# Block sums of the second layer's FFN weights: formed one layer earlier and kept in DRAM

## The chip, the cores and the metric

One core of a Trainium2 chip. The time of a run is in microseconds (us) of device time. TensorE (PE) multiplies; its weight loads stand as PEld. VectorE (DVE) and GpSimd (POOL) do elementwise work, ScalarE (ACT) copies, converts and evaluates functions, and SyncE (SP) issues all transfers of this kernel, in the order of its queue.

## The reference, cut to what matters

Two layers over 512 latent tokens and 256 context tokens of width 1024, all in float32. A layer is token mixing (four groups of heads) and a SwiGLU FFN of hidden width 2816; the context stream runs only in the first layer's FFN. The change is about the FFN of the second layer, for the latent tokens:

```
def swiglu(h, w_in_, w_out_):
    gate, up = jnp.split(h @ w_in_, 2, axis=-1)
    return (jax.nn.silu(gate) * up) @ w_out_
...
x = x + g_f * rms_norm(swiglu(modulate(rms_norm(x, norm_g[2]), sh_f, sc_f), w_ffn_in, w_ffn_out), norm_g[3])
```

`w_ffn_in` is 1024 x 5632 per layer, `w_ffn_out` 2816 x 1024. The vectors `sh_f`, `sc_f` and their like come from six products of the conditioning with `w_mod` (the modulation).

## The kernel before, in words

Features lie on the 128 partitions and tokens on the free axis. Every weight tile is split into a rounded part `wh` (ACT, line 408) and its remainder `wl` (POOL or DVE, line 409), activations likewise, and one block product is three matmuls (`mac3`, lines 470 to 472: wh with high, wh with low, wl with high). A weight unit is 128 x 1024 numbers (512 KB): `weights` (line 414) calls `tick`, takes a raw tile from the ring `wr` (5 buffers), issues its load on SP (line 425) and splits it in two halves into the rings `wh` and `wl` (5 buffers each). The 2816 hidden columns are 22 blocks j of 128, each with a gate tile (u = 0) and an up tile (u = 1) in `wfi`.

First layer, latent tokens (`ffn`): chunks of 8, 7 and 7 blocks; per block two units, then 8 units of `w_ffn_out` (wfo) per chunk, the last 6 of the last chunk in halves of the tokens. Beside it run background tasks: `mix` (line 1907) fills the queue `bg` with 32 tasks of `mods_sums` (the second layer's modulation, line 659: a 512 KB load at line 667 and two DVE operations at line 675 or 677 each) and sets `bg_rate` to `rate2`; each `tick` adds the rate and runs a task whenever a whole one has come together. What is left is flushed when the layer's last normalisation begins.

Second layer, latent tokens (`ffn_seven`): blocks 0 to 3 go as above; the other 18 are made by `strassen_pair` (line 1541). It takes the gate and up columns of a block as the two rows, and the two halves of the 1024 inputs as the two columns, of a 2 x 2 block matrix A = (a11 a12; a21 a22) of 128 x 512 each, and the two halves of the tokens and inputs as the other matrix. In place of eight block products it makes seven, with the sums of A formed on the spot from the two raw tiles (line 1553, helper `tt`): s1 = a21 + a22 and a21 = a11 - a21 on POOL, s2 = s1 - a11 and a12 = a12 - s2 on DVE (`sad` is 'PPVV'). Products 0, 2, 4 and 6 add into one PSUM tile, Z; between them Z is read, by ACT after product 0 (line 1579) and 2 (line 1583) and by DVE after product 4 (line 1587, tile `fd`). The sums of the other matrix are made once, in `strassen_rhs` (lines 1513 to 1539). Each product's block is split into wh and wl as it comes.

The chunks of blocks in the second layer are (0, 4), (4, 7), (7, 11), (11, 16) and (16, 22). While a chunk's products run, the 8 output tiles of the chunk before (`ffn_tiles`, wfo units from the ring `wq` of 2) are put between them; before, they are spread evenly: after each product, as many are made as keep step.

The order in which each engine's instructions run is set when the kernel is built, by a planner that goes by program order as priority and by its own estimates of durations; the engines then keep that order and wait on semaphores. Tiles of the arena (`main.get`) are 67 slots that are handed on in the order in which they are freed.

Of the kernel before, what the change touches and what calls it, by code (L numbers as in the profile page):

```python
# [11 lines left out]
F32 = mybir.dt.float32  # L12
# [5 lines left out]
ALU = mybir.AluOpType  # L18
# [3 lines left out]
P = 128  # L22
D = 1024
KT = D // P
# [3 lines left out]
HID = 22  # L28
# [9 lines left out]
 'netmp': 3,  # L38
 'nmain': 36,
 'nctx': 26,  # L40
 'wr': 5,
 'wh': 5,
 'wl': 5,
 'fcx': ((0, 8), (8, 15), (15, 22)),
# [19 lines left out]
 'latei': 2,  # L64
 'rate0': 0.8,
 'rate1': 0.2,
 'rate2': 0.5,
 'lo': ('4', '4', '6', '3', '2', '4', '5', '3', '4'),
 'sqk': 'VPVPVPVP',
 'sqe': 'AAAAAAAA',  # L70
# [38 lines left out]
 'strassen': (1,),  # L109
 'fcs': ((0, 4), (4, 7), (7, 11), (11, 16), (16, 22)),  # L110
 'fco': 4,
 'wq': 2,
 'sad': 'PPVV',
 'slo': 'PVVPPVP',
# [1 line left out]
 'srt': 'VPVP',  # L116
 'srl': 'VPVP',
 'sup': 'V',
 'sgl': 'V',
 'ws': 4}  # L120
UNIT = 1024
HALF = 544
NEG = -1e30
# [139 lines left out]
class Build:  # L263
    def __init__(self, tc, es, I, out, dbg=None):
        self.tc, self.nc, self.I, self.out, self.dbg = tc, tc.nc, I, out, dbg
        pool = lambda name, **k: es.enter_context(tc.tile_pool(name=name, **k))
        self.cp = pool("const", bufs=1)
        self.pp = pool("param", bufs=1)
        self.sp = pool("small", bufs=1)
        self.wr = pool("wr", bufs=T["wr"])  # L270
        self.wh = pool("wh", bufs=T["wh"])
        self.wl = pool("wl", bufs=T["wl"])
        self.ws = pool("ws", bufs=T["ws"])
# [12 lines left out]
        self.modrow = Arena(self.sp, "modrow", 1)  # L286
        self.bg = deque()
        self.pre = deque()
# [1224 lines left out]
    def strassen_rhs(self, h):  # L1513
# [24 lines left out]
        h.blocks = [[b11], [b21, b22]]  # L1538
        return out, [b11, b21, out[1], out[0], out[2], b22, out[3]]

    def strassen_pair(self, l, j, h, rhs, g, jj):

        nc = self.nc
        n = h.half
        raw = []
        for u in range(2):
            self.tick()
            r = self.wr.tile([P, UNIT], F32, tag="wr", name=self.name("wr"))
            nc.sync.dma_start(out=r.rearrange("p (a b) -> p a b", a=KT), in_=self.I["wfi"][l, j, u])
            raw.append(r)  # L1550
        a11, a12, a21, a22 = raw[0][:, 0:512], raw[0][:, 512:1024], raw[1][:, 0:512], raw[1][:, 512:1024]
        s1, s2 = (self.ws.tile([P, 512], F32, tag="ws", name=self.name("ws")) for _ in range(2))
        tt = lambda c, o, a, b, op: self.e(c).tensor_tensor(out=o, in0=a, in1=b, op=op)  # L1553
        ad = T["sad"]
        tt(ad[0], s1, a21, a22, ALU.add)
        tt(ad[1], a21, a11, a21, ALU.subtract)
        tt(ad[2], s2, s1, a11, ALU.subtract)
        lhs = [a11, a12, s2, s1, a21, a12, a22]
        z, w, y = self.mm(), None, None
        c1 = self.ar.temp("fc", 2 * n)  # L1560
        c2 = self.ar.temp("fd", n)
        e = self.ar.temp("fe", 2 * n)
        p5 = self.ar.temp("ff", n)
        c1t, c2t, p1, q, p5t = c1.t[:, 0:2 * n], c2.t[:, 0:n], e.t[:, 0:n], e.t[:, n:2 * n], p5.t[:, 0:n]
        for i in range(7):
# [2 lines left out]
            self.split(hi, lo, lhs[i], eng=self.e(T["slo"][i]))  # L1568
            if i == 1:
                y = self.mm()  # L1570
                tt(ad[3], a12, a12, s2, ALU.subtract)
# [26 lines left out]
        tt(T["sup"], a[:, n:2 * n], a[:, n:2 * n], c2t, ALU.mult)  # L1598
# [18 lines left out]
    def ffn_seven(self, l, st, h, G, chunks, first, hold, last, hold2, then, between, after):  # L1617
# [3 lines left out]
        n = st.n  # L1621
# [27 lines left out]
        for ci, (k0, k1) in enumerate(rest):  # L1649
            outs = self.ffn_tiles(l, y, g, j0, j1, KT, n, sq, ci == 0, False, self.mx)  # L1650
            ahead = 0 if ci else T["fco"]
            for _ in range(ahead):
                next(outs)
            gn = HL(self.ar, "g", k1 - k0, n)
            total, done = 7 * (k1 - k0), 0
            for i, _ in enumerate(self.strassen_tiles(l, k0, k1, h, rhs, gn)):
                while done * total < (i + 1) * (KT - ahead):
                    next(outs)
                    done += 1
            self.all(outs)  # L1660
            g.free()
            g, j0, j1 = gn, k0, k1
# [162 lines left out]
    def run(self):  # L1825
# [81 lines left out]
        def mix():  # L1907
            self.ar = side
            self.ctx_states(C, pn)
            main.absorb(side)  # L1910
            main.other, self.tmp.lends = self.tmp, True
            self.ar = main
            self.mods_sums(1, (2, 4, 3, 5), pn, 1)
            self.bg_rate = T["rate2"]

        self.layer_end(0, X, p, pn, norm, proj, mix)
# [162 lines left out]
```

## Time and profile before

| what | value |
|---|---|
| median of 3 runs | 1700.4 us (1699.37 to 1701.58) |
| the profiled execution | 1700.72 us |
| its span, first to last instruction | 1698.9 us |
| PE, DVE, ACT, POOL busy | 95%, 65%, 46%, 44% of the span |
| moved by DMA | 219.41 MB, mean 129 GB/s |
| chain that ended last | PE 13%, DVE 3%, issue 2%, POOL 2%, ACT 1% |

The profile is one execution. Busy time is the union of an engine's instructions; matmuls are pipelined and overlap in it. A wait is idle time of an engine ahead of an instruction, put down to what released it. The name left of an arrow is the tile that is written, right of it what is read; L is the line in the kernel. The first layer's FFN for the latent tokens runs from some 645 to 1046 us, the second layer's from 1311 us to the end, its seven products from some 1371 to 1657 us.

### The profile page before, as it was taken

What the parts mean: (1) busy time and instruction counts of PE and PEld (TensorE: products, weight loads), DVE (VectorE), ACT (ScalarE), POOL (GpSimd) and SP (SyncE); (2) the same over time, 40 slices, a digit from 0 to 9 for tenths busy, and PEclk for the clock granted to TensorE, in tenths of its full rate; (3) what the DMA queues carried; (4) which work ended last, traced back from release to release, by engine and by line L of the source; (5) the groups of instructions that cost most, each with busy time, mean ns of one, the idle gap of its engine ahead of it and who ended that gap; (6) DMA issues with size and microseconds to landing.
All of it is one profiled execution on the core that took longest, in us unless ns stands there. A gap on an engine that the chain in (4) does not pass through costs nothing. (4 is left out here: it accounts for less than half of the span.)

```text
span 1698.9 us, 28931 instructions
## 1 busy us (share of the span) xinstructions
PE 1605.5 (95%) x10616; PEld 1402.3 (83%) x10616; DVE 1095.9 (65%) x2330; ACT 787.5 (46%) x1782; POOL 748.9 (44%) x779
## 2 busy tenths in 40 slices
PE   6999998999999998999999997999698999999997
PEld 2976777887899998888888887999478988889886
DVE  4876675758785668643443556758756857677874
ACT  3655356554345545333322333464465344444451
POOL 2431334554466555322222224332425766676663
PEclk9999999899999999999999998999799999999998
DMA  9654553354475323344434453121032123333242
GB/s 312 228 174 160 202 192 118 109 174 153 124 246 180 122 87 102 125 148 137 140 122 147 148 188 97 54 75 63 1 125 88 63 80 97 105 106 106 77 124 69
DMA packets 85663, 219.41 MB, mean 129 GB/s; under 512 B 11025, under 2 KB 20113, under 8 KB 85521
## 3 DMA queue, kind: packets, MB, share of 16 engines
q1 hardware_dynamic: 85520, 217.57, 39.6%
q8 instruction: 83, 1.36, 0.3%
q14 instruction: 60, 0.48, 0.1%
HBM read 211.24 MB, written 6.29 MB: 128 GB/s over the span
## 5 line engine op out<-in xcount | busy, mean ns | idle before, releaser
L409 POOL TENSOR_TENSOR wl<-wr,wh 128x512 fp32r<-128x512 f32 (+2 forms) x250 | 335.9, 1349 | 505.6 <-ACT wh L408 487.3
L408 ACT ACTIVATE wh<-wr 128x512 fp32r<-128x512 f32 (+3 forms) x512 | 310.4, 617 | 452.6 <-PE mm L471 320.5
L409 DVE TENSOR_TENSOR wl<-wr,wh 128x512 fp32r<-128x512 f32 (+3 forms) x262 | 218.7, 838 | 127.5 <-ACT wh L408 125.5
L470 PE MATMUL mm<-hfh_m,wh 128*128 128x512 f32 (+1 forms) x320 | 125.0, 391 | 0.0
L472 PE MATMUL mm<-hfh_m,wl 128*128 128x512 f32 (+1 forms) x320 | 124.8, 390 | 0.0
L471 PE MATMUL mm<-hfl_m,wh 128*128 128x512 f32 (+1 forms) x320 | 124.5, 389 | 0.0
L471 PE MATMUL mm<-hfl_c,wh 128*128 128x256 f32 x352 | 100.8, 287 | 0.6 <-POOL hfl_c L582 0.6
L472 PE MATMUL mm<-hfh_c,wl 128*128 128x256 f32 x352 | 100.6, 286 | 0.0
L470 PE MATMUL mm<-hfh_c,wh 128*128 128x256 f32 x352 | 100.1, 285 | 0.0
L472 PEld LDWEIGHTS mm<-hfh_m,wl 128*128 128x128 f32 x320 | 60.5, 189 | 13.5
L471 PEld LDWEIGHTS mm<-hfl_m,wh 128*128 128x128 f32 x320 | 60.4, 189 | 13.0
L470 PEld LDWEIGHTS mm<-hfh_c,wh 128*128 128x128 f32 x352 | 66.7, 190 | 5.3 <-issue 2.3
L470 PEld LDWEIGHTS mm<-hfh_m,wh 128*128 128x128 f32 x320 | 60.4, 189 | 12.9
L471 PEld LDWEIGHTS mm<-hfl_c,wh 128*128 128x128 f32 x352 | 66.8, 190 | 2.0 <-POOL hfl_c L582 0.8
L472 PEld LDWEIGHTS mm<-hfh_c,wl 128*128 128x128 f32 x352 | 67.0, 190 | 1.6 <-issue 0.6
L677 DVE SCALAR_TENSOR_TENSOR macc_m<-wr,cs,macc_m 128x512 f32<-128x512 f32 x56 | 43.0, 767 | 29.6 <-DMA wr<-in_wmod_dram 28.6
L471 PE MATMUL mm<-gl_m,wh 128*128 128x512 f32 x152 | 59.8, 394 | 0.0
L472 PE MATMUL mm<-gh_m,wl 128*128 128x512 f32 x152 | 59.7, 394 | 0.0
L470 PE MATMUL mm<-gh_m,wh 128*128 128x512 f32 x152 | 59.6, 396 | 0.0
L470 PE MATMUL mx<-gh_m,wh 128*128 128x512 f32 x128 | 50.7, 399 | 3.3 <-ACT wh L408 2.2
L472 PE MATMUL mx<-gh_m,wl 128*128 128x512 f32 x128 | 50.9, 398 | 1.6 <-POOL wl L409 1.2
L471 PE MATMUL mx<-gl_m,wh 128*128 128x512 f32 x128 | 50.5, 394 | 0.0
(725 smaller groups left out, 5420.9 us busy)
## 6 DMA issues: line engine op xcount, KB each, us to landing
wr<-in_wfi_dram SPq DMA_DIRECT2D x132, 512.0 KB, 3.8
wr<-in_wmod_dram SPq DMA_DIRECT2D x80, 512.0 KB, 4.1
wr<-in_wT_dram SPq DMA_DIRECT2D x42, 512.0 KB, 3.9
wr<-in_wo_dram SPq DMA_DIRECT2D x24, 512.0 KB, 3.9
wr<-in_wfo_dram SPq DMA_DIRECT2D x24, 512.0 KB, 4.0
wm_m<-in_wmod_dram SPq DMA_DIRECT2D x32, 256.0 KB, 5.2
wr<-in_wfo_dram SPq DMA_DIRECT2D x16, 448.0 KB, 3.8
wr<-in_wfo_dram SPq DMA_DIRECT2D x16, 384.0 KB, 3.4
```

The costliest lines, as they stand in the source:

```text
L408: nc.scalar.activation(hi, src, AF.Copy)
L409: (eng or nc.vector).tensor_tensor(out=lo, in0=src, in1=hi.bitcast(F32), op=ALU.subtract)
L470: nc.tensor.matmul(out, lh, rh, start=first, stop=False, skip_group_check=more)
L471: nc.tensor.matmul(out, lh, rl, start=False, stop=False, skip_group_check=more)
L472: nc.tensor.matmul(out, ll, rh, start=False, stop=last, skip_group_check=more)
L677: nc.vector.scalar_tensor_tensor(out=t, in0=w, scalar=self.cs[:, k, s:s + 1], in1=t, op0=ALU.mult, op1=ALU.add)
```

## The change

The first layer's FFN gets 36 more background tasks (`weight_sums`), put evenly among the 32 of the modulation, and `rate2` is 1.4 in place of 0.5. A task loads the four 128 x 512 blocks of a hidden block j (four transfers of 256 KB into arena slots), or forms the four sums (as before two on POOL and two on DVE) and stores them to a DRAM tile (four transfers of 256 KB); the load of j + 1 stands ahead of the forming of j. In the second layer a pair loads four tiles: a11 and a12 (512 KB), s2 and s1, a21 and a12 from DRAM (512 KB each) and a22 (256 KB), in the order in which the products use them, and forms nothing. The ring `wr` has 7 buffers in place of 5; the ring `ws` of the sums (4 buffers of half the size) goes. The output tiles between the products stand at fixed places: a pair that is due one has it behind product 5, a second one behind product 1, a third behind product 3.

```
--- before.py
+++ after.py
@@ -38,7 +38,7 @@
  'netmp': 3,
  'nmain': 36,
  'nctx': 26,
- 'wr': 5,
+ 'wr': 7,
  'wh': 5,
  'wl': 5,
  'fcx': ((0, 8), (8, 15), (15, 22)),
@@ -64,7 +64,7 @@
  'latei': 2,
  'rate0': 0.8,
  'rate1': 0.2,
- 'rate2': 0.5,
+ 'rate2': 1.4,
  'lo': ('4', '4', '6', '3', '2', '4', '5', '3', '4'),
  'sqk': 'VPVPVPVP',
  'sqe': 'AAAAAAAA',
@@ -109,6 +109,7 @@
  'strassen': (1,),
  'fcs': ((0, 4), (4, 7), (7, 11), (11, 16), (16, 22)),
  'fco': 4,
+ 'fcp': (5, 1, 3),
  'wq': 2,
  'sad': 'PPVV',
  'slo': 'PVVPPVP',
@@ -116,8 +117,7 @@
  'srt': 'VPVP',
  'srl': 'VPVP',
  'sup': 'V',
- 'sgl': 'V',
- 'ws': 4}
+ 'sgl': 'V'}
 UNIT = 1024
 HALF = 544
 NEG = -1e30
@@ -270,7 +270,6 @@
         self.wr = pool("wr", bufs=T["wr"])
         self.wh = pool("wh", bufs=T["wh"])
         self.wl = pool("wl", bufs=T["wl"])
-        self.ws = pool("ws", bufs=T["ws"])
         self.wq = pool("wq", bufs=T["wq"])
         self.ap = pool("arena", bufs=1)
         self.dr = pool("dram", bufs=1, space=bass.MemoryType.DRAM)
@@ -285,6 +284,7 @@
         self.ar = self.main
         self.modrow = Arena(self.sp, "modrow", 1)
         self.bg = deque()
+        self.sums = {}
         self.pre = deque()
         self.bg_rate = self.bg_acc = 0.0
         self.uid = 0
@@ -1538,24 +1538,54 @@
         h.blocks = [[b11], [b21, b22]]
         return out, [b11, b21, out[1], out[0], out[2], b22, out[3]]
 
+    def weight_sums(self, l, j0, j1):
+
+        nc = self.nc
+
+        def load(j, box):
+            for u in range(2):
+                for v in range(2):
+                    s = self.main.get("sa")
+                    nc.sync.dma_start(out=s.t[:, 0:512].rearrange("p (a b) -> p a b", b=P), in_=self.I["wfi"][l, j, u][:, v * 4:v * 4 + 4])
+                    box.append(s)
+
+        def form(j, box):
+            a11, a12, a21, a22 = (s.t[:, 0:512] for s in box)
+            box += [self.main.get("sb") for _ in range(2)]
+            s1, s2 = (s.t[:, 0:512] for s in box[4:])
+            tt = lambda c, o, a, b, op=ALU.subtract: self.e(c).tensor_tensor(out=o, in0=a, in1=b, op=op)
+            e = T["sad"]
+            tt(e[0], s1, a21, a22, ALU.add)
+            tt(e[1], a21, a11, a21)
+            tt(e[2], s2, s1, a11)
+            tt(e[3], a12, a12, s2)
+            d = self.dr.tile([P, 2, KT, P], F32, tag=f"ws{l}{j}", name=f"ws{l}{j}")
+            self.sums[l, j] = d
+            for i, x in enumerate((s2, s1, a21, a12)):
+                nc.sync.dma_start(out=d[:, i // 2, i % 2 * 4:i % 2 * 4 + 4], in_=x.rearrange("p (a b) -> p a b", b=P))
+            for s in box:
+                s.free()
+
+        boxes = {j: [] for j in range(j0, j1)}
+        tasks = [lambda: load(j0, boxes[j0])]
+        for j in range(j0, j1):
+            if j + 1 < j1:
+                tasks.append(lambda j=j: load(j + 1, boxes[j + 1]))
+            tasks.append(lambda j=j: form(j, boxes[j]))
+        return tasks
+
     def strassen_pair(self, l, j, h, rhs, g, jj):
 
         nc = self.nc
         n = h.half
         raw = []
-        for u in range(2):
+        for src in (self.I["wfi"][l, j, 0], self.sums[l, j][:, 0], self.sums[l, j][:, 1], self.I["wfi"][l, j, 1][:, KT // 2:KT]):
             self.tick()
             r = self.wr.tile([P, UNIT], F32, tag="wr", name=self.name("wr"))
-            nc.sync.dma_start(out=r.rearrange("p (a b) -> p a b", a=KT), in_=self.I["wfi"][l, j, u])
+            k = src.shape[1]
+            nc.sync.dma_start(out=r[:, 0:k * P].rearrange("p (a b) -> p a b", a=k), in_=src)
             raw.append(r)
-        a11, a12, a21, a22 = raw[0][:, 0:512], raw[0][:, 512:1024], raw[1][:, 0:512], raw[1][:, 512:1024]
-        s1, s2 = (self.ws.tile([P, 512], F32, tag="ws", name=self.name("ws")) for _ in range(2))
-        tt = lambda c, o, a, b, op: self.e(c).tensor_tensor(out=o, in0=a, in1=b, op=op)
-        ad = T["sad"]
-        tt(ad[0], s1, a21, a22, ALU.add)
-        tt(ad[1], a21, a11, a21, ALU.subtract)
-        tt(ad[2], s2, s1, a11, ALU.subtract)
-        lhs = [a11, a12, s2, s1, a21, a12, a22]
+        lhs = [r[:, i * 512:i * 512 + 512] for r in raw for i in range(2)][0:7]
         z, w, y = self.mm(), None, None
         c1 = self.ar.temp("fc", 2 * n)
         c2 = self.ar.temp("fd", n)
@@ -1568,7 +1598,6 @@
             self.split(hi, lo, lhs[i], eng=self.e(T["slo"][i]))
             if i == 1:
                 y = self.mm()
-                tt(ad[3], a12, a12, s2, ALU.subtract)
             if i == 3:
                 w = self.mm()
             ps, first = [(z, True), (y, True), (z, False), (w, True), (z, False), (w, False), (z, False)][i]
@@ -1595,7 +1624,7 @@
         nc.scalar.activation(a, c1t, AF.Tanh)
         nc.vector.scalar_tensor_tensor(out=a, in0=a, scalar=1.0, in1=c1t, op0=ALU.add, op1=ALU.mult)
         nc.vector.tensor_tensor(out=a[:, 0:n], in0=z[:, 0:n], in1=a[:, 0:n], op=ALU.mult)
-        tt(T["sup"], a[:, n:2 * n], a[:, n:2 * n], c2t, ALU.mult)
+        self.e(T["sup"]).tensor_tensor(out=a[:, n:2 * n], in0=a[:, n:2 * n], in1=c2t, op=ALU.mult)
         self.split(g.h[jj], g.l[jj], a, eng=self.e(T["sgl"]))
         for x in (c1, c2, e):
             x.free()
@@ -1652,11 +1681,11 @@
             for _ in range(ahead):
                 next(outs)
             gn = HL(self.ar, "g", k1 - k0, n)
-            total, done = 7 * (k1 - k0), 0
+            nj, left = k1 - k0, KT - ahead
             for i, _ in enumerate(self.strassen_tiles(l, k0, k1, h, rhs, gn)):
-                while done * total < (i + 1) * (KT - ahead):
+                q = (i // 7 + 1) * left // nj - i // 7 * left // nj
+                if i % 7 in T["fcp"][0:q]:
                     next(outs)
-                    done += 1
             self.all(outs)
             g.free()
             g, j0, j1 = gn, k0, k1
@@ -1911,6 +1940,10 @@
             main.other, self.tmp.lends = self.tmp, True
             self.ar = main
             self.mods_sums(1, (2, 4, 3, 5), pn, 1)
+            a, b = list(self.bg), self.weight_sums(1, T["fcs"][0][1], HID)
+            self.bg.clear()
+            for i, f in enumerate(b):
+                self.bg += a[i * len(a) // len(b):(i + 1) * len(a) // len(b)] + [f]
             self.bg_rate = T["rate2"]
 
         self.layer_end(0, X, p, pn, norm, proj, mix)
```

## Rows read from the trace of the kernel before

**Rows 1.** Page: busy time with share and count; GB/s in forty slices.

```profile
PE 1605.5 (95%) x10616; PEld 1402.3 (83%) x10616; DVE 1095.9 (65%) x2330; ACT 787.5 (46%) x1782; POOL 748.9 (44%) x779
...
GB/s 312 228 174 160 202 192 118 109 174 153 124 246 180 122 87 102 125 148 137 140 122 147 148 188 97 54 75 63 1 125 88 63 80 97 105 106 106 77 124 69
```

**Rows 2.** Stages: us; PE, PEld, DVE, ACT, POOL busy (x); PEclk, DMA share, GB/s.

```profile
20.00:30.00 10.00, 8.94 (x47) 3.51 (x45) 5.99 (x19) 1.18 (x4) 2.64 (x7) 1.00 1.05 403
800.00:900.00 100.00, 100.00 (x442) 81.42 (x441) 42.79 (x62) 30.67 (x52) 23.71 (x18) 1.00 0.42 137
900.00:1000.00 100.00, 100.00 (x441) 81.45 (x441) 48.44 (x71) 32.85 (x58) 25.13 (x19) 1.00 0.47 152
1360.00:1376.00 16.00, 13.03 (x70) 10.01 (x69) 10.06 (x10) 6.32 (x12) 11.89 (x9) 1.00 0.32 99
1376.00:1460.00 84.00, 81.79 (x578) 75.91 (x577) 56.37 (x75) 42.87 (x86) 51.07 (x38) 1.00 0.29 89
1460.00:1560.00 100.00, 96.38 (x680) 89.42 (x679) 71.89 (x97) 46.59 (x91) 68.85 (x47) 1.00 0.34 105
1560.00:1660.00 100.00, 96.71 (x654) 88.04 (x653) 75.28 (x96) 48.25 (x98) 62.61 (x44) 1.00 0.35 103
```

**Rows 3.** Waits of PE, 1360 to 1660 us: total us, times, longest.

```profile
PE mm L470 <- DVE fd_m L1587: 4.2, 5, 1.2
PE mx L470 <- ACT wh L408: 2.2, 2, 1.6
```

**Rows 4.** Waits of PE, 690 to 1010 us: the only one.

```profile
PE mx L1329 <- POOL kw_c L304: 0.2, 1, 0.2
```

**Rows 5.** Timeline, 1478 to 1483 us: start, us, operation, [idle before <- its releaser].

```profile
1478.76 1.30 POOL L1553 TENSOR_TENSOR ws<-wr 128x512 f32<-128x512 f32 x1 [1.15 <-DMA wr<-in_wfi_dram]
...
1480.09 1.76 DVE L1553 TENSOR_TENSOR ws<-ws,wr 128x512 f32<-128x512 f32 x1 [3.23 <-POOL ws L1553]
...
1481.77 0.41 DVE L1587 TENSOR_TENSOR fd_m<-mm,fd_m 128x256 f32<-128x256 f32 x1
...
1482.23 0.19 PEld L470 LDWEIGHTS mm<-st3h_m,wh 128*128 128x128 f32 x1 [1.38 <-DVE fd_m L1587]
```

**Rows 6.** Line 1553, the sums: ns min/median/max; then what they waited for (us, times).

```profile
L1553 POOL TENSOR_TENSOR ws<-wr x18: 1282/1292/1746, 1312.5 to 1616.5; 128x512 f32<-128x512 f32 x18
...
L1553 DVE TENSOR_TENSOR ws<-ws,wr x18: 676/1752/1784, 1314.0 to 1617.8; 128x512 f32<-128x512 f32 x18
...
L1553 POOL TENSOR_TENSOR wr<-wr,wr x18: 1342/1738/1803, 1315.2 to 1619.0; 128x512 f32<-128x512 f32 x18
...
L1553 DVE TENSOR_TENSOR wr<-wr,ws x18: 674/1038/1780, 1377.3 to 1634.0; 128x512 f32<-128x512 f32 x18
...
  POOL ws L1553: 33.4, 13
...
  DMA wr<-in_wfi_dram: 17.3, 13
```

**Rows 7.** Timeline of PE around 1408 us.

```profile
1407.61 0.28 PE L471 MATMUL mm<-hf10l_m,wh 128*128 128x256 f32 x1
1407.73 0.28 PE L472 MATMUL mm<-hf10h_m,wl 128*128 128x256 f32 x1
1408.59 0.38 PE L470 MATMUL mm<-st3h_m,wh 128*128 128x256 f32 x1 [0.59 <-DVE fd_m L1587]
```

**Rows 8.** DMA issues by line: count, KB each, median us to landing.

```profile
wr<-in_wfi_dram SPq DMA_DIRECT2D x132, 512.0 KB, 3.8
...
xs<-x_m SPq DMA_DIRECT2D x8, 256.0 KB, 2.1
```

**Rows 9.** SP queue: modulation loads of line 667 (first and last start); sixteen issues.

```profile
L667 SPq DMA_DIRECT2D wr<-in_wmod_dram x32: 378/378/379, 655.7 to 1000.8; - x32
...
2.57 10.38 SPq L627 DMA_DIRECT2D wm_m<-in_wmod_dram  x16
```

**Rows 10.** Waits of PE, 1010 to 1320 us: the second in size.

```profile
PE mx L1431 <- DVE ht_m L800: 7.8, 3, 3.4
```

More of the change, by code (lines that the diff above doesn't have):

```diff
@@ L40 @@
  'nctx': 26,
- 'wr': 5,
+ 'wr': 7,
  'wh': 5,
@@ L111 @@
  'fco': 4,
+ 'fcp': (5, 1, 3),
  'wq': 2,
@@ L118 @@
  'sup': 'V',
- 'sgl': 'V',
- 'ws': 4}
+ 'sgl': 'V'}
 UNIT = 1024
@@ L287, in __init__ @@
         self.bg = deque()
+        self.sums = {}
         self.pre = deque()
@@ L1539, in strassen_rhs, with weight_sums, load, form @@
         return out, [b11, b21, out[1], out[0], out[2], b22, out[3]]
+    def weight_sums(self, l, j0, j1):
+        nc = self.nc
+        def load(j, box):
+            for u in range(2):
+                for v in range(2):
+                    s = self.main.get("sa")
+                    nc.sync.dma_start(out=s.t[:, 0:512].rearrange("p (a b) -> p a b", b=P), in_=self.I["wfi"][l, j, u][:, v * 4:v * 4 + 4])
+                    box.append(s)
+        def form(j, box):
+            a11, a12, a21, a22 = (s.t[:, 0:512] for s in box)
+            box += [self.main.get("sb") for _ in range(2)]
+            s1, s2 = (s.t[:, 0:512] for s in box[4:])
+            tt = lambda c, o, a, b, op=ALU.subtract: self.e(c).tensor_tensor(out=o, in0=a, in1=b, op=op)
+            e = T["sad"]
+            tt(e[0], s1, a21, a22, ALU.add)
+            tt(e[1], a21, a11, a21)
+            tt(e[2], s2, s1, a11)
+            tt(e[3], a12, a12, s2)
+            d = self.dr.tile([P, 2, KT, P], F32, tag=f"ws{l}{j}", name=f"ws{l}{j}")
+            self.sums[l, j] = d
+            for i, x in enumerate((s2, s1, a21, a12)):
+                nc.sync.dma_start(out=d[:, i // 2, i % 2 * 4:i % 2 * 4 + 4], in_=x.rearrange("p (a b) -> p a b", b=P))
+            for s in box:
+                s.free()
+        boxes = {j: [] for j in range(j0, j1)}
+        tasks = [lambda: load(j0, boxes[j0])]
+        for j in range(j0, j1):
+            if j + 1 < j1:
+                tasks.append(lambda j=j: load(j + 1, boxes[j + 1]))
+            tasks.append(lambda j=j: form(j, boxes[j]))
+        return tasks
     def strassen_pair(self, l, j, h, rhs, g, jj):
@@ L1545, in strassen_pair @@
         raw = []
-        for u in range(2):
+        for src in (self.I["wfi"][l, j, 0], self.sums[l, j][:, 0], self.sums[l, j][:, 1], self.I["wfi"][l, j, 1][:, KT // 2:KT]):
             self.tick()
             r = self.wr.tile([P, UNIT], F32, tag="wr", name=self.name("wr"))
-            nc.sync.dma_start(out=r.rearrange("p (a b) -> p a b", a=KT), in_=self.I["wfi"][l, j, u])
+            k = src.shape[1]
+            nc.sync.dma_start(out=r[:, 0:k * P].rearrange("p (a b) -> p a b", a=k), in_=src)
             raw.append(r)
[L1551 to L1558, printed above, removed]
+        lhs = [r[:, i * 512:i * 512 + 512] for r in raw for i in range(2)][0:7]
         z, w, y = self.mm(), None, None
@@ L1597, in strassen_pair @@
         nc.vector.tensor_tensor(out=a[:, 0:n], in0=z[:, 0:n], in1=a[:, 0:n], op=ALU.mult)
-        tt(T["sup"], a[:, n:2 * n], a[:, n:2 * n], c2t, ALU.mult)
+        self.e(T["sup"]).tensor_tensor(out=a[:, n:2 * n], in0=a[:, n:2 * n], in1=c2t, op=ALU.mult)
         self.split(g.h[jj], g.l[jj], a, eng=self.e(T["sgl"]))
@@ L1654, in ffn_seven @@
             gn = HL(self.ar, "g", k1 - k0, n)
-            total, done = 7 * (k1 - k0), 0
+            nj, left = k1 - k0, KT - ahead
             for i, _ in enumerate(self.strassen_tiles(l, k0, k1, h, rhs, gn)):
-                while done * total < (i + 1) * (KT - ahead):
+                q = (i // 7 + 1) * left // nj - i // 7 * left // nj
+                if i % 7 in T["fcp"][0:q]:
                     next(outs)
-                    done += 1
             self.all(outs)
@@ L1913, in mix @@
             self.mods_sums(1, (2, 4, 3, 5), pn, 1)
+            a, b = list(self.bg), self.weight_sums(1, T["fcs"][0][1], HID)
+            self.bg.clear()
+            for i, f in enumerate(b):
+                self.bg += a[i * len(a) // len(b):(i + 1) * len(a) // len(b)] + [f]
             self.bg_rate = T["rate2"]
```

4 lines of the change are left out of this document (1 added, 3 removed).

## The prediction

> **What bounds the kernel now.** I read the page first: TensorE (PE) is busy for 1605.5 of 1698.9 us [rows 1], so time comes off only where PE waits, and an engine beside it matters only where it makes PE wait. The stages say where that is [rows 2]. In the first layer's FFN (800 to 1000 us stand for it) PE is busy 100 of 100 us, VectorE (DVE) 43 and 48, GpSimd (POOL) 24 and 25, and the DMA engines move 137 and 152 GB/s; PE's waits from 690 to 1010 us add up to 0.2 us [rows 4]. In the seven products (1376 to 1660) PE is busy 81.79 of 84, 96.38 of 100 and 96.71 of 100 us, with POOL at 61 to 69% and DVE at 67 to 75%; the 16 us ahead, where the products begin, hold 2.97 us of idle PE.
>
> The waits of PE there (the two largest of 9 rows, which hold sixteen waits and 11.9 us) [rows 3] end in `fd_m` (L1587, DVE's read of the Z sum, without which product 6 may not add to Z), in `wl` halves from POOL, and in ScalarE (ACT). One of them in full [rows 5]: POOL's first sum starts at 1478.76 when its weight block lands; DVE has stood 3.23 us for it with its next sum; that sum takes 1.76 us; only then comes `fd_m`, ready long before, and PE's last product has waited 1.38 us. DVE stood 33.4 us in 13 such places, and POOL 17.3 us for the blocks themselves [rows 6]. So the stage is not short of throughput: a late weight block holds POOL, POOL holds DVE, and work for PE stands in line behind both.
>
> A wait counts from the end of the matmul before, and that end is modelled: matmuls start 0.12 us apart with 0.28 us each, and the one behind the wait at 1408.59 started 0.86 us after its forerunner, with 0.59 counted [rows 7]. Each wait thus costs about 0.15 us more than its row: 11.9 + 16 x 0.15 = 14.3 us of the stage. That is the pool a gain must come from.
>
> **The sums leave the seven products.** 18 pairs lose two POOL sums (1.29 and 1.74 us) and two on DVE (medians 1.75 and 1.04) each [rows 6]: 18 x 3.03 = 55 us of POOL and 18 x 2.79 = 50 us of DVE, nearly all of them in the 284 us from 1376 on, so POOL falls from 64% to about 46% and DVE from 72% to about 55%. What counts is the order: nothing left in DVE's queue waits for POOL to form something, and nothing in POOL's waits for a weight block to land; the blocks go to ACT alone.
>
> *Waits behind 1376 us.* PE's idle is 2.21 + 3.62 + 3.29 = 9.1 us [rows 2], with about 13 restarts of 0.15 it is 11.1 us. With 13 places where DVE stood for POOL's sum [rows 6] against about 13 waits of PE, a sum stands ahead of most of them; what stays is ACT's share. I take 8 tenths: 8.9 us. Bounds: all 11.1, or 4.2 alone (the `fd_m` row).
>
> *Waits ahead of 1376 us*, 2.97 + 0.45 = 3.4 us: here the right-hand side's own sums and a late second-layer weight hold the engines, and only one pair's sums are among them. A third: 1.1 us; bounds 0 and 3.4.
>
> *Fixed places.* The wfo tiles go behind products 5, 1 and 3. Products 6, 2 and 4 are those that add to Z and so wait for a read of Z; an output tile of 12 to 15 matmuls (2.8 to 3.5 us) now stands in front of each. That covers the `fd_m` waits, the longest of which is 1.2 us, and I count it inside the 8 tenths, not on top. PE's own work is the same.
>
> *More to load.* A pair reads 1.75 MB in place of 1.0 (MiB), four transfers in a ring of 7 instead of two in 5. That is 18 x 0.79 MB = 14 MB over 284 us: 105 + 50 = 155 GB/s, about what the first layer's FFN runs at without a wait [rows 2, 4]. A 512 KB block lands in 3.8 us [rows 8]; seven slots hold 1.75 pairs of 284 / 18 = 15.8 us. Cost 0; if the ring were short, one landing per pair would show, which is rival 2.
>
> **What the first layer's FFN gets.** 36 tasks (18 loads of four 256 KB blocks, 18 formings of four sums and four stores) join 32 modulation tasks, at 1.4 per weight unit instead of 0.5. 68 / 1.4 = 49 units of the 62 in the stretch, so all is formed before its end; before, 32 / 0.5 = 64 ran to the very end (the last modulation load is issued at 1000.8 [rows 9]). A unit is 24 matmuls, or 21 for the shorter second chunk: 49 units are some 1150 matmuls, at 100 us / 441 [rows 2] 261 us. In these:
> - DVE: 36 sums of 0.68 to 1.78 us [rows 6], 24 to 64 us or 9 to 24%, beside the 46% it has, and 3% as the modulation work is squeezed by a quarter: 58 to 73%.
> - POOL: 36 sums of 1.28 to 1.80 us, 46 to 65 us: 18 to 25% beside its 25%, 43 to 50%.
> - The SP queue: 144 more transfers. Sixteen of 256 KB were issued in 10.38 us, 0.65 each [rows 9]: 94 us; with the 81 it has, 146 of 261. SP takes its orders in turn, and each store waits for its sum; weight loads stand behind it. A sum follows its blocks by about four tasks (three units, 16 us), so SP should hang on the chain of the four sums at worst, some 5 us.
> - DMA: weights 25.2 MB, modulation 16.8, blocks 18.9, stores 18.9: 79.8 MB in 261 us = 305 GB/s, where about 145 ran before. The most that this trace shows is 403 GB/s, and that in 256 KB transfers from 20 to 30 us [rows 2]. Stores of 256 KB land in 2.1 us [rows 8].
>
> The cover for all of this is the lead of the weight halves: five `wl` buffers of 12 matmuls, 13.6 us, plus the loaded blocks in the ring. PE's 0.2 us of waits show it whole. None of the four comes to 100%, so I cost the layer at 1 us; bounds: a gain of 1 (modulation work no longer runs into the layer's end, where its last load was issued at 1000.8 [rows 9]) and a loss of 14 if the cover ran out once in full.
>
> By the Trainium skill ("SBUF — State Buffer", section "SBUF: two separate sides") a DVE operation with two SBUF inputs and a POOL operation exclude each other for the whole instruction. The trace agrees: the same DVE sum takes 0.68 us at least and 1.75 in the median [rows 6]. By that rule the new POOL sums could block DVE for all of their 46 to 65 us, 18 to 25% on top of its own work; even that leaves DVE under 100% and, with the cover, PE's time as it is.
>
> **Elsewhere.** The build orders every engine's instructions anew, and the ring of 7 lets weights run further ahead in all stages. No row prices that. The nearest is a wait in the second layer's mixing, 7.8 us in 3 pieces [rows 10]: one such wait more or less is 2.6 us either way. I take 0.
>
> **Sum.** The profiled execution took 1700.7 us (span 1698.9 and 1.8 around it); the median of the runs is 0.3 lower, at 1700.4. 1700.7 - 8.9 - 1.1 + 1 = 1691.7, and 0.3 lower as a median: **1691 us**. Its own range: gains of 4.2 to 14.5, a loss or gain of 1 in the first layer and 2.6 for order: 1685 to 1698.
>
> **Rivals.**
> 1. *The FFN of the first layer becomes DMA-bound (slower).* Place: 700 to 960 us, SP's queue. It decides from 79.8 MB / (261 + 13.6) us = 291 GB/s: if loads and stores mixed run below that, weights come late by 79.8 MB / rate - 274.6 us. At 270 GB/s that is 21 us: 1691 + 21 = **1712**; at 246, the highest slice of the page behind the first [rows 1], 50 us. For it: no row shows loads and stores mixed for 260 us, and SP in order ties each load to the sums. Against it: 403 GB/s. The Trainium skill ("SBUF — State Buffer", section "The DMA setup-cost knee") gives 224 GB/s for 256 KiB transfers; by that figure the 37.7 MB of blocks and stores take 168 us, and the other 42 MB at the trace's 403 GB/s 104: 272 us, at the very edge of this rival. The trace disagrees where it can, with 403 GB/s in loads of that size.
> 2. *The waits move on and little is gained.* ACT must now take every half from a ring that two transfers per two products fill, and `wl` from POOL still takes 1.3 to 1.7 us behind ACT's 0.6. The gain is then one fourth of the pool, 3 us, less 1 in the first layer: **1699**. For it: `ACT wh` has 2.2 us of PE's waits today [rows 3]. Against it: ACT is busy for about half of the stage [rows 2].
> 3. *The relief is whole:* all 14.3 us of the pool, and 2.6 us by order: 1700.4 - 16.9 = **1683.5**. For it: POOL and DVE fall to half. Against it: the beginning of the stage has other causes.
> 4. *The sums aren't formed in the cover* (the tasks run out late and are flushed at the layer's end, where PE waits on DVE): 62 units x 1.4 = 87 tasks against 68 speak against it; it would cost like rival 1 and shares its chance.
>
> **How the numbers follow.** Forecast 0.62, rival 1 (with 4) 0.14, rival 2 0.13, rival 3 0.11. A measurement can tell 0.2%, 3.4 us. Faster: 0.59 of the forecast's 0.62, rival 3, and 0.04 of rival 2: 0.74. Same: 0.03 + 0.09 + 0.01 of rival 1: 0.13. Slower: 0.13. The range 1684 to 1702 leaves out rival 1 beyond its first us and half of rival 3.
>
> **What would show it.** Right: in the stage of the seven products POOL near 46%, DVE near 54%, PE's waits for `fd_m` gone and all its waits below 4 us; the first layer's FFN with PE at 100% and DMA near 300 GB/s until about 960 us, then near 90. Wrong: PE waiting for weight halves between 700 and 960 us with DMA landings far above 4 us (rival 1); or the seven products with as much idle PE behind ACT's `wh` (rival 2). A change of over 5 us outside of both stages would say that the order did it.

## The result, and the profile after

The changed kernel takes **1688.4 us** in the median of 4 runs (1688.17 to 1689.32), the kernel before 1700.6 beside it: ratio 0.9929, 95% interval 0.9912 to 0.9947. The forecast was 1691. The profiled execution has a span of 1687.2 us where it had 1698.9.

The seven products first, since the forecast rests on them. These are the stretches of the changed kernel (us; PE, PEld, DVE, ACT, POOL busy; PEclk, DMA share, GB/s), with two short ones around 766 us that the text comes to:

```profile
750.00:766.00 16.00, 8.72 (x40) 6.78 (x39) 9.38 (x14) 3.86 (x8) 2.66 (x2) 0.94 0.46 138
766.00:773.00 7.00, 6.98 (x21) 5.67 (x22) 6.35 (x7) 2.24 (x4) 5.11 (x3) 0.64 0.94 321
...
800.00:900.00 100.00, 100.00 (x446) 81.56 (x445) 73.92 (x86) 30.62 (x52) 50.42 (x34) 1.00 0.89 311
900.00:1000.00 100.00, 100.00 (x446) 81.56 (x445) 55.01 (x74) 31.54 (x54) 38.97 (x29) 1.00 0.67 226
...
1360.00:1376.00 16.00, 14.47 (x89) 11.91 (x87) 10.57 (x12) 5.51 (x10) 11.08 (x8) 1.00 0.31 98
1376.00:1460.00 84.00, 83.27 (x591) 77.88 (x591) 41.09 (x65) 46.63 (x89) 37.29 (x30) 1.00 0.48 152
1460.00:1560.00 100.00, 100.00 (x728) 94.49 (x727) 55.19 (x87) 52.47 (x97) 44.40 (x34) 1.00 0.52 163
1560.00:1660.00 100.00, 100.00 (x696) 92.97 (x695) 57.21 (x91) 48.95 (x97) 46.16 (x35) 1.00 0.42 130
```

Against [rows 2]: behind 1376 us PE's idle time has gone from 9.1 us to 0.73; the 16 us ahead have 1.53 us where they had 2.97. PE's waits from 1360 to 1660 us are these four and no more (total us, times, longest), where [rows 3] stood for sixteen:

```profile
PE mx L470 <- ACT wh L408: 0.7, 1, 0.7
PE mx L471 <- DVE gl_m L412: 0.7, 1, 0.7
PE mx L472 <- POOL wl L409: 0.6, 1, 0.6
PE mx L470 <- ACT gh_m L411: 0.2, 1, 0.2
```

In the first layer's FFN PE had one wait of 0.2 us [rows 4]. Now, from 690 to 1010 us, it has these:

```profile
PE mm L470 <- ACT gh_m L411: 6.2, 1, 6.2
PE mm L472 <- DVE wl L409: 1.1, 1, 1.1
```

To see where time came and went, take one matmul that both kernels have and compare when it starts. Rows of the tiles `gh_m` and `hxh_m` in both traces (count; ns min/median/max; first and last start, us), first the kernel before:

```profile
L470 PE MATMUL mm<-gh_m,wh x152: 387/393/479, 757.2 to 1660.7; 128*128 128x512 f32 x152
...
L470 PE MATMUL mm<-gh_m,wt_m x144: 274/280/368, 1011.4 to 1683.6; 128*128 128x256 f32 x144
...
L470 PE MATMUL mx<-gh_m,wh x128: 387/394/504, 1363.5 to 1641.1; 128*128 128x512 f32 x128
...
L492 PE MATMUL mm<-hxh_m,wh x144: 274/281/388, 1097.3 to 1190.4; 128*128 128x256 f32 x144
```

and the kernel after:

```profile
L470 PE MATMUL mm<-gh_m,wh x152: 388/394/792, 754.3 to 1649.3; 128*128 128x512 f32 x152
...
L470 PE MATMUL mm<-gh_m,wt_m x144: 275/281/365, 1017.9 to 1671.9; 128*128 128x256 f32 x144
...
L470 PE MATMUL mx<-gh_m,wh x128: 387/394/504, 1366.9 to 1632.2; 128*128 128x512 f32 x128
...
L492 PE MATMUL mm<-hxh_m,wh x144: 274/281/390, 1099.3 to 1192.4; 128*128 128x256 f32 x144
```

Five starts cut the run into five parts: the first output tile of the first layer's FFN (757.2 before), the first of that FFN's last output tiles, which are made in halves (first `wt_m` matmul, 1011.4), the second layer's projections (`hxh_m`, 1097.3), the first of the four output tiles that stand ahead of the seven products (`mx`, 1363.5), and the last `wt_m` matmul of all (1683.6). The lengths of the parts, worked out from these rows and from the same rows of every experiment (the last column is the start that closes the fifth part):

```
us                to first  first FFN  norm and     to the    the seven    last
                  out tile  out tiles  projections  products  products    start
before              757.2     254.2       85.9       266.2      320.1     1683.6
after               754.3     263.6       81.4       267.6      305.0     1671.9
e1_even             751.6     264.0       81.3       267.5      306.3     1670.7
e2_ring5            752.8     256.5       86.9       265.7      304.3     1666.2
e3_noform           753.4     254.0       80.1       266.4      304.3     1658.2
e4_before_fixed     756.2     254.2       86.9       267.7      334.8     1699.8
e5_noform_ring5     754.6     254.2       86.7       265.2      304.8     1665.5
s1_split            752.4     259.8       81.4       268.4      304.5     1666.5
s2_rate             753.8     260.6       81.7       265.7      304.8     1666.6
s3_inplace          757.2     256.5       81.5       267.6      305.0     1667.8
s4_actq             751.5     259.0       81.4       267.6      304.6     1664.1
s5_actq_inplace     753.8     268.6       81.4       267.3      304.6     1675.7
m1_ahead            753.2     261.3       82.1       267.1      304.0     1667.7
m2_ahead_split      754.3     254.8       81.4       268.4      304.9     1663.8
```

After against before: -2.9, +9.4, -4.5, +1.4, -15.1, in sum -11.7. So there are three effects, not one: the seven products give 15 us, the first layer's FFN takes 9, and the way into the second layer gives 4.5, which the forecast had at nothing. Each row of the table is one execution. The first part runs from 751.5 to 757.2 us, and those two ends are two kernels that both have 7 buffers; so its -2.9 is within what such parts differ by in any case. The third part splits cleanly, 80.1 to 82.1 or 85.9 to 86.9.

The 9 us lie in one place. This is the chain of waits of the changed kernel that ends at 766.02 us (start, us, what), its short pieces left out:

```profile
728.88 1.75 POOL sb_m L1556
...
730.64 0.33 SPq L1565
...
731.53 5.47 DMA ws<-sb_m
...
737.16 1.31 POOL sb_m L1556
...
738.56 1.30 POOL sa_m L1556
...
739.88 5.34 DMA ws<-sa_m
...
745.24 0.33 SPq L1549
...
745.67 4.70 DMA wr<-in_wmod_dram
...
752.44 4.19 DMA wr<-in_wmod_dram
...
758.98 3.62 DMA wr<-in_wmod_dram
...
763.35 0.69 DVE wl L409
...
764.70 0.61 DVE ft_m L1508
...
765.34 0.64 ACT gh_m L411
...
766.02 0.79 PE mm L470
```

Read it downwards. A sum on GpSimd ends and its store leaves; the next pair's first sum wants that same slot and waits the 5.47 us of the store; its second sum is stored; a load (L1549) wants that slot and waits 5.34 us; SP, which takes its orders in turn, gives out the modulation load behind it only then. VectorE stands for this block and for the next two, each given out only when VectorE frees a buffer, and behind them in its queue stand the weight half and the gate that PE needs. At 100 us for 446 matmuls (800 to 900 us), the 16 us to 766 should hold 71 matmuls and hold 40, which is 7 us; and the 7 us after it run at a granted clock of 0.64, part of them at the lower of the two levels (1.2 GHz), with 21 matmuls in place of 31, another 2.3 us.

### The profile page after: what moved, and what is told of

Same layout as the page of the kernel before. It is cut to its first block, busy times and chain, and to the rows that moved or that the text cites. A ratio compares the mean times of both kernels' runs of the same rounds, so it can differ in the third digit from the quotient of the medians.

```text
span 1687.2 us, 29374 instructions
## 1 busy us (share of the span) xinstructions
PE 1604.0 (95%) x10616; PEld 1401.4 (83%) x10616; DVE 1089.6 (65%) x2330; ACT 791.9 (47%) x1782; POOL 739.8 (44%) x779
## 4 chain that ended last, share of the span: by engine, by line
PE 82%; DVE 10%; DMA 3%; issue 2%; ACT 1%; POOL 1%; SPq 0%; DVEq 0%; POOLq 0%; ACTq 0%
PE mm L470 19%; PE mm L471 19%; PE mm L472 19%; PE ms L634 2%; PE mx L471 2%; PE mx L472 2%; PE mx L1147 2%; PE mx L470 2%; PE mm L487 1%; PE mm L634 1%; PE mx L1399 1%; PE mm L488 1%; PE mm L492 1%; PE mx L1141 1%; PE mm L493 1%
## 5 line engine op out<-in xcount | busy, mean ns | idle before, releaser
L409 POOL TENSOR_TENSOR wl<-wr,wh 128x512 fp32r<-128x512 f32 (+2 forms) x268 | 361.3, 1353 | 439.7 <-ACT wh L408 387.5
L408 ACT ACTIVATE wh<-wr 128x512 fp32r<-128x512 f32 (+3 forms) x548 | 333.5, 617 | 438.6 <-PE mm L471 299.6
L409 DVE TENSOR_TENSOR wl<-wr,wh 128x512 fp32r<-128x512 f32 (+3 forms) x280 | 225.3, 807 | 124.8 <-ACT wh L408 120.7
L677 DVE SCALAR_TENSOR_TENSOR macc_m<-wr,cs,macc_m 128x512 f32<-128x512 f32 x56 | 59.0, 1054 | 19.4 <-DMA wr<-in_wmod_dram 18.7
L470 PEld LDWEIGHTS mm<-hfh_m,wh 128*128 128x128 f32 x320 | 60.2, 188 | 12.9
L411 ACT ACTIVATE gh_m<-ft_m 128x512 fp32r<-128x512 f32 (+1 forms) x32 | 17.6, 551 | 77.1 <-DVE ft_m L1508 77.1
```

The lines of the kernel that those rows point to most:

```text
L408: nc.scalar.activation(hi, src, AF.Copy)
L409: (eng or nc.vector).tensor_tensor(out=lo, in0=src, in1=hi.bitcast(F32), op=ALU.subtract)
L411: nc.scalar.activation(hi, src, AF.Copy, scale=scale)
L470: nc.tensor.matmul(out, lh, rh, start=first, stop=False, skip_group_check=more)
L677: nc.vector.scalar_tensor_tensor(out=t, in0=w, scalar=self.cs[:, k, s:s + 1], in1=t, op0=ALU.mult, op1=ALU.add)
```

## The experiments

Theory A, after the result: the gain of the seven products comes from the sums having left them; the first layer's FFN pays for the forming by that chain; the ring of 7 is worth some 5 us at the start. Rival: the fixed places make the gain.

**The places undone** (`e1_even`):

```diff
-            nj, left = k1 - k0, KT - ahead
+            total, done = 7 * (k1 - k0), 0
...
-                q = (i // 7 + 1) * left // nj - i // 7 * left // nj
-                if i % 7 in T["fcp"][0:q]:
+                while done * total < (i + 1) * (KT - ahead):
                     next(outs)
+                    done += 1
```

> The changed kernel with one part undone: the output tiles of the group before are again spread evenly over the products, not put behind products 5, 1 and 3. Theory A (the seven-products stage is quicker because the sums have left VectorE and GpSimd, not because of the places): 1688 to 1692 us, the seven-products stage still 273 to 276 us long, and no PE wait for fd_m above 2 us in sum. Rival P (the places take the waits for the sums of products away): 1693 to 1698 us, with fd_m waits of 4 us or more back behind 1377 us.

1687.7 us, ratio 0.9929 (0.9917 to 0.9942), the same as the change itself; the fifth part is 306.3 us, and no wait for `fd_m` is left. The places are worth nothing once the sums are gone.

**The places alone** (`e4_before_fixed`: the kernel before, with the new loop and `'fcp': (5, 1, 3)`, nothing else):

> The kernel before with one part of the change alone: output tiles at the fixed places behind products 5, 1 and 3 of a block pair, the sums still formed beside the products, 5 buffers in the ring. Theory A (the waits come from the load of the sums on VectorE and GpSimd, the places only move them): 1698 to 1702 us, the seven-products stage 286 to 290 us. Rival P (the places give the gain): 1690 to 1694 us, the stage near 280 us or below. Rival Q (they cover the fd_m waits of 4.2 and 5 us at most): 1695 to 1697 us.

1714.9 us, ratio 1.0089 (1.0074 to 1.0104): **slower by 15 us**, which none of the three had. Nearly all of it is in the fifth part, 334.8 us where it was 320.1. PE's five largest waits there, 1360 to 1660 us (line numbers one higher than in [rows 3]):

```profile
PE mm L471 <- ACT fe_m L1580: 7.5, 3, 2.9
PE mm L473 <- DVE wl L410: 4.4, 4, 2.1
PE mx L473 <- DVE wl L410: 2.8, 5, 1.2
PE mx L471 <- ACT wh L409: 2.4, 3, 1.5
PE mm L471 <- DVE fd_m L1588: 1.4, 1, 1.4
```

`fd_m` did fall, from 4.2 us [rows 3] to 1.4, as the tiles in front of the adding products should make it. But ACT's read of Z (`fe_m`) and the halves that DVE forms late took its place, with more than was won: DVE still stands for POOL's sums, 39.9 us in 11 places where it was 33.4 in 13 [rows 6].

**The ring at 5** (`e2_ring5`: `'wr': 5` for 7):

> The changed kernel with 5 buffers in the ring of weight loads (wr) where it has 7. Theory A (7 buffers are worth some 5 us in the first 100 us, where the kernel before had PE waits near 66, 85 and 95 us, and nothing later): 1692 to 1694 us, PE busy in 80 to 120 us back near 36.4 us of 40, the seven-products stage unchanged at 273 us. Rival N (the start is given back later by the waits that follow): 1688 to 1689 us. Rival R (7 buffers also cover the loads of the seven products): 1696 us or more, with new PE waits behind 1377 us.

**1681.9 us**, ratio 0.9895 (0.9881 to 0.9909): faster than the change, where each theory had it slower or equal. The start was given back as rival N has it: the first `hxh_m` matmul of the first layer starts at 99.1 us with 7 buffers and 104.6 with 5, but the first output tile at 754.3 and 752.8, and the fifth part is unchanged: the seven products don't need the ring of 7. But the second part is 256.5 us in place of 263.6, and PE's waits in 690 to 1010 us are one:

```profile
PE mm L472 <- POOL wl L409: 0.8, 1, 0.8
```

Against it, the third part is 86.9 us where the ring of 7 has 81.4.

**No forming, with either ring** (`e3_noform`, and `e5_noform_ring5` with `'wr': 5` as well):

```diff
- 'rate2': 1.4,
+ 'rate2': 0.5,
...
-        for src in (self.I["wfi"][l, j, 0], self.sums[l, j][:, 0], self.sums[l, j][:, 1], self.I["wfi"][l, j, 1][:, KT // 2:KT]):
+        for src in (self.I["wfi"][l, j, 0], self.I["wfi"][l, j, 1], self.I["wfi"][l, j, 0], self.I["wfi"][l, j, 1][:, KT // 2:KT]):
...
-            a, b = list(self.bg), self.weight_sums(1, T["fcs"][0][1], HID)
-            self.bg.clear()
-            for i, f in enumerate(b):
-                self.bg += a[i * len(a) // len(b):(i + 1) * len(a) // len(b)] + [f]
```

> The changed kernel with the forming of the sums left out: no loads, sums or stores for them in the first layer's FFN, the background's rate back at 0.5, and the seven products read weight blocks as they lie in the input, of the same shapes and sizes (so the sums are left out of the computation). Theory A (forming costs the first layer's FFN some 6 us net, a stall near 750 us of 11.8 less 5.4 regained near 1050): 1681 to 1684 us with no PE wait above 1 us in 690 to 960 us, and the earlier end of the modulation's matmuls (963.6 us) lost again. Rival C (forming is free, the 6 us belong to the order of the instructions): 1687 to 1690 us. Rival D (forming costs its whole stall, the gain near 1050 us comes from elsewhere): 1675 to 1678 us.

> The forming left out as in the kernel without forming before (raw blocks of the same sizes in the products, so the sums are left out of the computation), and the ring of weight loads at 5. With 5 buffers and forming 1681.9 us was measured, with 7 and without it 1675.5, with both 1687 to 1688. Theory S (forming costs time only where its chain of slots and stores meets the ring of 7 near 750 us; a ring of 7 is by itself worth about 6 us, at 75 to 100 us and near 1040 us): 1680 to 1682 us, that is, forming is free with 5 buffers. Rival K (forming has a price of 5 us or more of its own in any ring): 1675 to 1677 us.

1675.5 us, ratio 0.9857 (0.9841 to 0.9874), and 1683.0 us, 0.9903 (0.9887 to 0.9920). With the two kernels that form the sums this is a square:

```
us            formed   not formed   forming costs
ring of 5     1681.9     1683.0         -1.1
ring of 7     1688.4     1675.5        +12.9
7 for 5 gives   -6.5       +7.5
```

With 5 buffers forming is free (the intervals of the first row overlap). It costs 13 us together with the ring of 7, 9.6 of them in the second part of the run. And without forming the ring of 7 is worth 7.5 us, most of it in the third part (80.1 us against 86.7): every kernel with 5 buffers has 85.9 to 86.9 us there, every one with 7 has 80.1 to 82.1. So my reason for the third part in `e3_noform` (an earlier end of the modulation's work) was wrong: without forming the last of its loads is given out at 990.6 us, 54 us later than in the changed kernel, and the part is the shortest of all. PE's waits for the normalisation there (1010 to 1100 us), before:

```profile
PE ms L554 <- DVE sq_t L529: 7.2, 1, 7.2
PE ms L554 <- DVE sq_m L529: 1.0, 1, 1.0
PE ms L554 <- POOL sq_m L529: 1.0, 1, 1.0
```

In the changed kernel only `sq_t` of the three is left, with 5.5 us; with 5 buffers and the sums formed (`e2_ring5`) it is `sq_t` with 5.5 and DVE's `sq_m` with 2.4.

**What in the chain makes the stall?** Four of its links, each loosened alone in the kernel with 7 buffers. Theory S: slots that are used again behind a store; W: SP's waits for the sums it must store; H: as W, with the stores on another queue; M: VectorE standing for modulation blocks just given out.

*Slower tasks* (`s2_rate`: `'rate2': 1.15` for 1.4).

> The changed kernel with the background's rate at 1.15 tasks per weight unit where it has 1.4: the 68 tasks then take 59 of the 62 units, a pair's sums every 17.5 us in place of 14.4. Theory S (a chain of load 5.5, sums 3 to 5, store 5.3 us in the same slots fills the 14.4 us; slower tasks leave it room): 1676 to 1681 us, and PE's wait near 766 us of 6.2 us gone or below 1. Rival O (slots are short at three pairs whatever the rate, or the stall comes with the order): 1686 to 1689 us with a wait of 4 us or more.

*Fewer slots* (`s3_inplace`):

```diff
-            box += [self.main.get("sb") for _ in range(2)]
-            s1, s2 = (s.t[:, 0:512] for s in box[4:])
+            s1, s2 = a22, a11
```

> The changed kernel with the first two sums written over blocks that are no longer read (A21 + A22 over A22, the second sum over A11), so that a pair takes 4 slots in place of 6. As the kernel is built, no slot is left at the pairs formed near 750 us, and each load there takes a slot whose store has just been given out; with 4 slots two more are free. Theory S (the stall is that reuse behind a store): 1676 to 1680 us, no PE wait above 2 us in 690 to 1020 us. Rival W (it is SP, which stands for the sums ahead of its stores, and that stays): 1685 to 1689 us.

*Stores as a task of their own* (`s1_split`):

```diff
-            for i, x in enumerate((s2, s1, a21, a12)):
-                nc.sync.dma_start(out=d[:, i // 2, i % 2 * 4:i % 2 * 4 + 4], in_=x.rearrange("p (a b) -> p a b", b=P))
-            for s in box:
+            for s in (box[0], box[3]):
                 s.free()
+        def store(j, box):
+            d = self.sums[l, j]
+            for i, s in enumerate((box[5], box[4], box[2], box[1])):
+                nc.sync.dma_start(out=d[:, i // 2, i % 2 * 4:i % 2 * 4 + 4], in_=s.t[:, 0:512].rearrange("p (a b) -> p a b", b=P))
+                s.free()
...
             tasks.append(lambda j=j: form(j, boxes[j]))
+            tasks.append(lambda j=j: store(j, boxes[j]))
```

> The changed kernel with the four stores of a pair as a task of their own behind its sums (86 tasks, rate 1.7 for the same 51 units), and the slots of A11 and A22 given back with the sums. Rival W (SP stands for the sums ahead of its stores, 14 waits on POOL's and 26 on DVE's sums, 50 us in all, and loads of weights and modulation stand behind it): 1676 to 1680 us, SP's waits for the sums below 10 us. Theory S (slots are what is short): 1683 to 1688 us, since the slots of the two other blocks come free later than now.

Rate 1683.7 us (0.9901, 0.9882 to 0.9919), slots 1684.9 (0.9916, 0.9896 to 0.9936), split 1682.5 (0.9887, 0.9868 to 0.9906). Each takes some of the stall and none all: the 6.2 us wait at 766 is gone in all three, and shorter ones stand elsewhere (690 to 1020 us: 3.4 us in all, 2.3 and 3.8, each in three waits). By the time alone only the split is clear of the change, whose interval is 0.9912 to 0.9947; the two others overlap with it. None of the theories is borne out alone. In the split version SP's waits for sums didn't fall below 10 us as W has it; on the two of `sb` alone it stands 56 us, where the changed kernel has 38.6 (690 to 1010 us):

```profile
SPq L1570 <- POOL sb_m L1556: 33.5, 13, 5.4
SPq L1570 <- DVE sb_m L1556: 22.5, 14, 3.5
```

*Stores on ScalarE's queue*, in `s1_split` (`s4_actq`) and with the slots saved as well (`s5_actq_inplace`):

```diff
-                nc.sync.dma_start(out=d[...
+                nc.scalar.dma_start(out=d[...
```

> As the kernel with the stores in a task of their own (1682.5 us), but the 72 stores are given out by ScalarE's queue, not SP's. Theory H (each store in SP's queue waits for a sum that VectorE and GpSimd form at the present unit, so SP loses its lead of several units there, and the loads behind it land late and hold VectorE and GpSimd): SP's waits for sums are gone, PE waits in 690 to 1000 us below 1 us, and the time falls to 1676 to 1678 us, near the 1675.5 us without forming. Rival S (slots that wait for their stores): 1681 to 1684 us. Rival A (stores in ScalarE's queue hold the weight halves that it rounds): 1684 us or more, with PE waits for wh.

> The same with the sums written over the blocks (4 slots a pair in place of 6). Theory H: 1675 to 1678 us, as with 6 slots, for slots are no longer what loads wait for. Rival S: 1676 to 1678 us while the version with 6 slots stays at 1681 or more. Rival A: 1684 us or more in both.

1681.2 us (0.9893, 0.9868 to 0.9918) and 1691.1 (0.9945, 0.9923 to 0.9966). The first is no better than the split on SP's queue: now ACT stands for the sums ahead of the weight halves it owes. Its waits, 690 to 1010 us:

```profile
ACT wh L408 <- DVE sb_m L1556: 27.6, 4, 10.9
...
ACT wh L408 <- POOL sa_m L1556: 11.8, 2, 6.4
```

So the wait changed queues, and rival A is right about its kind. That the second loses 10 us more, 268.6 us in its second part, with PE waits of 8.2 us in all, no theory had, and it stays open.

*Modulation loads one task earlier* (`m1_ahead` in the changed kernel, `m2_ahead_split` in `s1_split`):

```diff
         def pair(part, i, k0, acc):
-            raw = self.wr.tile([P, UNIT], F32, tag="wr", name=self.name("wr"))
-            c = slice(i * 512, i * 512 + 512)
-            nc.sync.dma_start(out=raw.rearrange(...
+            if not raws:
+                fetch()
+            fetch()
+            raw = raws.popleft()
```

(`fetch` gives out the load of the next pair in the list and appends its buffer to `raws`.)

> The changed kernel with each modulation load given out one task ahead of the task that uses it (ring of 7, rate 1.4, nothing else changed). Theory M (PE's wait near 766 us comes by VectorE, which stands for modulation blocks given out just before, 18.7 us in 6 places from 690 to 960 us, and forms the weight halves and the gate late): 1677 to 1681 us, VectorE's waits for those blocks below 8 us, PE's waits in 690 to 1000 us below 2 us. Rival S (the loads stand in SP's queue behind a load that waits for a store's slot, and being one task earlier doesn't help): 1685 to 1689 us with a PE wait of 4 us or more.

> The kernel with the stores in a task of their own on SP's queue (1682.5 us), with the modulation loads one task ahead as well. Theory M: 1676 to 1680 us, near the 1675.5 us without forming. Rival S, or a price that forming has wherever its stalls are moved: 1681 to 1684 us, with PE waits of 2 to 4 us in 850 to 960 us as in the version without the earlier loads.

1684.4 us (0.9907, 0.9890 to 0.9923) and **1679.2 us** (0.9879, 0.9864 to 0.9894). Alone it does what the others do (PE's waits are 3.4 us in two, and the interval overlaps with the change's); VectorE's waits for these blocks fall from 18.7 us to 13.3, not below 8. With the split its second part is 254.8 us, as long as that of the kernel before, which forms nothing there, and PE's waits from 690 to 1010 us are 1.2 us:

```profile
PE mx L1340 <- DVE C L1349: 0.8, 1, 0.8
PE mm L472 <- POOL wl L409: 0.4, 1, 0.4
```

while in 800 to 900 us of that kernel the transfers run faster than in any other:

```profile
800.00:900.00 100.00, 100.00 (x445) 81.63 (x445) 79.20 (x92) 29.91 (x52) 53.44 (x36) 1.00 0.95 333
```

This is the best version that forms the sums: quicker than the change (the intervals of the ratios are apart), in the median quicker than `e2_ring5` (they overlap, 0.9864 to 0.9894 against 0.9881 to 0.9909). Of the 12.9 us that forming cost with 7 buffers it gives 9 back.

## Why the prediction was right, point by point

**What bounds the kernel.** Right: the pool of 14.3 us in the seven products is what the change could take, and it took it (320.1 to 305.0 us). Every kernel in which the sums have left the products has 304.0 to 306.3 us there, whatever its ring, places or way of forming them.

**Waits behind and ahead of 1376 us.** The mechanism is right, POOL at 44 to 46% and DVE at 49 to 57% as forecast, `fd_m` gone; the size was too small, 10.0 us for 15.1. PE's idle time fell by 9.8 us (8.4 behind 1376 us, 1.4 ahead of it); the other 5.3 us lie in stretches in which PE counts as busy. Twelve restarts fewer at the prediction's 0.15 us are 1.8 of them; what the rest is no run shows. The 8 tenths kept ACT's share back, but PE's waits for `wh` fell from 2.2 us to 0.7 without ACT having less to do; that ACT, too, had been held by what stood still behind the sums is argued, not shown. Ahead of 1376 us, half of the idle time went where I took a third. Rival 3, the whole pool, was the truer term for this stage.

**Fixed places.** "That covers the `fd_m` waits", counted inside the 8 tenths: with the sums gone they cover nothing that is left (`e1_even`), and with the sums there they cost 15 us (`e4_before_fixed`). [rows 3] could have warned: `fd_m` is 4.2 us of PE's 11.9, and an output tile that is moved in front of one product no longer stands in front of another.

**More to load, cost 0.** Right: 130 to 163 GB/s behind 1376 us against 155 forecast, no landing shows as a wait of PE, and a ring of 5 does as well there.

**The first layer's FFN, cost 1.** Wrong in size: 9.4 us, inside the bounds (a loss of 14) and far from the value. The step that failed is "SP should hang on the chain of the four sums at worst, some 5 us", set against a cover of 13.6 us. I weighed each delay alone; in the run they stand in series, five transfers (23.3 us) in slots and buffers that wait for one another, 37 us from 728.88 to 766.02, and a store takes longer under this load (5.1 and 5.4 us) than the 2.1 that [rows 8] gave, a block of 256 KB 5.5:

```profile
sa_m<-in_wfi_dram SPq DMA_DIRECT2D x72, 256.0 KB, 5.5
...
ws<-sb_m SPq DMA_DIRECT2D x36, 256.0 KB, 5.4
...
ws<-sa_m SPq DMA_DIRECT2D x36, 256.0 KB, 5.1
```

The other parts of that step held. POOL's share of 50% and DVE's of 74% in 800 to 900 us stand at the upper ends of the forecasts, 43 to 50 and 58 to 73, or just above. The tasks ended early (the last modulation load at 936.1 us, before at 1000.8 [rows 9]), which was worth nothing in itself, as `e3_noform` shows:

```profile
L667 SPq DMA_DIRECT2D wr<-in_wmod_dram x32: 378/379/697, 638.2 to 936.1; - x32
```

**Rival 1** named the right place and half the mechanism (SP in order, loads tied to the sums), and its price by rate was wrong: the stretch isn't short of DMA rate. PE is at 100% at 311 GB/s here and at 333 in `m2_ahead_split`, in which nearly half of the bytes go in transfers of 256 KB. The Trainium skill ("SBUF — State Buffer", section "The DMA setup-cost knee") gives 224 GB/s for a transfer of 256 KiB; with many under way, of this and of double the size, the measured rate is higher, and the measurement decides.

**Elsewhere, 0.** Wrong by 6.0 us in sum (-2.9, -4.5, +1.4), and by the prediction's own sign ("a change of over 5 us outside of both stages would say that the order did it") something else was at work. For the -4.5 it is the ring of 7, whether by its buffers or by the order that the build makes with them; the -2.9 is no more than the first part differs by anyway. I took the ring for a part of the products' loads; it is a resource of all stages, and the square and the table show that its gain lies in the third part and its cost, with the forming, in the second.

**Sum.** Its own range of 1685 to 1698 doesn't add up all its bounds: with the 2.6 us for order it would be 1682 to 1700. And the forecast of 1691 came so near partly by luck, by errors that offset each other: 5 us too little gain in the products, 8 too little cost in the first FFN, 6 too little gain elsewhere.

**What stays open.** Why 5 buffers avoid the stall near 766 us. All three kinds of wait are in `e2_ring5` too, in like measure: from 690 to 1010 us SP stands 56.5 us for the sums that it must store, where the changed kernel has 52.9, and its block loads stand 10.1 us for stores, against 13.5. VectorE stands even longer for modulation blocks (690 to 960 us), in the changed kernel

```profile
DVE macc_m L677 <- DMA wr<-in_wmod_dram: 18.7, 6, 5.0
```

and in `e2_ring5`

```profile
DVE macc_m L677 <- DMA wr<-in_wmod_dram: 35.1, 13, 5.9
```

So none of these waits makes the stall by its total; it comes where they meet. The build plans every engine's order for the ring and the tasks that it is given, and the orders of SP and VectorE differ between these two kernels, so no run tells two more buffers from the order that comes with them, in the second part or in the third. For the same reason the four single cures suggest that the stall needs several links, but don't show it, and the shares of the links are not settled.

## What to carry to other kernels

When sums or loads are moved into a stage whose engines have room, add up the longest chain of transfers, slots and queues that wait for one another there, with the landing times under the new load; shares of busy time don't show it. A parameter that is changed along with the main edit (a ring's length here) has its own gain and its own cost in other stages: try the corners of the square, since the best one may be a version nobody asked for. A schedule tuned beside one change (the fixed places) can be worth nothing with it and be a loss without it.

## What the runs showed of the hardware

One wait of 6.2 us cost more than its length: the granted clock was 0.64 in the 7 us after it, 2.3 us more. And a transfer given out by ScalarE's queue holds that engine while it waits for its data (`s4_actq`, 690 to 1010 us): 39 us of waits for sums in front of `wh`, where the same stores had kept SP waiting.
